# A decoder layer in fp32 on one core: other order of the first loads, one more filler product, and another rank for head norms and rotations

## The chip, the core and the metric

The kernel runs on one core of a Trainium2 chip. The metric is device time in microseconds of one execution; a run gives one such time, and one execution is profiled with the hardware's trace. Of the kernel before there are three runs and one profiled execution. TensorE multiplies matrices (PE in the profile; its weight loads are PEld), VectorE is DVE, ScalarE is ACT, GpSimd is POOL, and SyncE (SP) issues most loads.

## The reference

One layer on 256 rows of width 1024, in float32: a norm, one wide projection into three attention branches and their gates, three attentions, their merge, and a feed-forward part with a causal convolution.

```python
h = rmsnorm(x, mix_norm_g[l])
proj = h @ w_in[l]
qa, ka, va, qd, kd, vd, qm, graw = jnp.split(proj, split_at, axis=-1)
qa = rope(rmsnorm(heads(qa, N_MOBA_HEADS), moba_q_norm_g[l]), positions)
ka = rope(rmsnorm(heads(ka, N_MOBA_HEADS), moba_k_norm_g[l]), positions)
...
gates = jax.nn.sigmoid(graw.astype(jnp.float32)).astype(x.dtype).reshape(B, S, N_BRANCHES, D_MODEL)
mem_n = rmsnorm(mem, mem_norm_g[l])
mkv = (mem_n @ w_mem_kv[l]).reshape(B, N_MEM, 2, N_MEM_HEADS, HEAD_DIM)
...
o_a = moba_attention(qa, ka, va).reshape(B, S, MOBA_W) @ w_branch_moba[l]
o_d = dilated_attention(qd, kd, vd).reshape(B, S, DIL_W) @ w_branch_dil[l]
o_m = memory_attention(qm, mk, mv).reshape(B, S, MEM_W) @ w_branch_mem[l]
merged = gates[:, :, 0] * o_a + gates[:, :, 1] * o_d + gates[:, :, 2] * o_m
x = x + merged @ w_out[l]
h2 = rmsnorm(x, ffn_norm_g[l])
u = causal_depthwise_conv(h2 @ w_ffn_up[l], ffn_conv_w[l], ffn_conv_b[l])
u_gate, u_val = jnp.split(u, 2, axis=-1)
x = x + (jax.nn.silu(u_gate) * u_val) @ w_ffn_down[l]
```

`qa`, `ka`, `va` and `qd`, `kd`, `vd` are 384 columns wide (six heads of 64), `qm`, `mk`, `mv` 256; `graw` is 3072 wide, which the kernel takes in twelve gates of 256 columns (G0 to G11).

## The kernel before

Every product is made of three: both operands are split into a rounded part (`hi`) and the rest (`lo`), and `mm3` adds hi x hi, hi x lo and lo x hi in PSUM. A weight piece of up to 1024 columns is loaded by SyncE into one of six raw buffers (`load`, `NRAW`), rounded on ScalarE (`split_hi`), and the rest is taken on VectorE, or on ScalarE and a GpSimd DMA (`split_lo`). The columns of x are handled alike: `column_task` scales one column block of 128 by the norm's gain, the hi on ScalarE, the lo on VectorE (tile `T_x`). The factor of the norm itself is applied later, to the products (`rs_x`, `R`).

The order of the work is made by a planner when the program is built, not by hand and not on the chip. The class `Order` (methods `run` and `issue`) keeps a clock for each engine with estimated costs; every piece of work is a generator that yields stages, and at each step the ready stage with the lowest rank on the next engine is written out. The chip then runs each engine's list in that order. Where TensorE would be idle by that clock for over half a microsecond early on, `keep_busy` fills the time with products of a tile of ones, which nobody reads (`warm_...`).

The projections stand in the order va, vd, qa, G0, ka, G1, G2, mv, mk, and so on (`ORDER`). A k is a block of 128 of the 1024 rows of a weight; va is loaded in pieces of 1, 1, 2, 2, 2 k (`CUTS` and pieces of at most two k), the other projections in four pieces of two k. Products go piece by piece, both row halves t = 0, 1 for each: 12 products for a piece of two k.

The head of the program is written in `tile_layer` from line 1120: `LOADS` lists the first transfers, `x01` for the x columns 0 and 1 excluded, `g` for `small` (gains and positions), `w` for the next weight piece. The x columns went out on ScalarE's queue, the rest on SyncE's. There are eight semaphores for such transfers, taken in turn, so a transfer also waits for the one eight before it.

After a q or k projection `post_task` (line 592) does the head norms and the rotation, for t = 0 and then t = 1: squares on ScalarE (`sq_qa`), sums and a scalar step on VectorE (`hs_qa`), a power on GpSimd, the rotation on VectorE (`t_qa`: a product with `ropeA`, two with `ropeB`, an addition). After both halves, for each t: the scaling on VectorE (a `SCALAR_TENSOR_TENSOR` on `t_qa`), three transposes on TensorE (`tp_qa`), a copy on ScalarE. The stages of one task follow in this order, so the scaling of half 0 stands behind the rotation of half 1. Its rank was 20. Splitting a weight ranks by how many units ahead it is needed (`PRIO_SPLIT` with `urgency`, line 389): 0 for three units, then 12, 12, 22, 35, 40. The sums of squares of the memory rows (`junk_mem`, `mem_rows_task`) rank 23.

```python
PRIO_SPLIT = (0, 0, 0, 12, 12, 22, 35, 40)
...
        for t in range(NT):
            t1, rs, _ = parts[t]
            yield Stage("dve")
            dve.scalar_tensor_tensor(t1, t1, rstd[src, t][:, 0:1], rs, op0=ALU.mult, op1=ALU.mult)
            rows = t1.rearrange("p h d -> p (h d)")
            yield Stage("pe", bank_free("tp"))
```

Of the kernel before, what the change touches and what calls it, by code (L numbers as in the profile page):

```python
# [25 lines left out]
DH = 64  # L26
# [10 lines left out]
WARM = 4  # L37
RAW = 3
PRIO_SCALE = 11
CUTS = (0, 1, 2, 4, 8)  # L40
LOADS = "x01 g w x12 w x24 w x48 w w w"
SUMS = (4, 130, 5)
BACK = (1.5, 2.0)
SLACK = 0.6
# [193 lines left out]
def tile_layer(ctx: ExitStack, tc: tile.TileContext, io, out):  # L238
    nc = tc.nc
    od = Order(nc)  # L240
# [186 lines left out]
    task = {}  # L427
# [324 lines left out]
    def post_start(nm, accs):  # L752
        w = WID[nm]
        src = "mem" if nm in ("mk", "mv") else "x"
        if nm in ("va", "vd", "mv"):
            res[nm] = apool.tile([P, NT, w], F32, tag="v_" + nm, name="v_" + nm)
            task[nm] = od.add(v_task(accs, res[nm], w, src), 10)
        else:
            kind = ("qa", "ka", "qd", "kd", "qm", "mk").index(nm)
            res[nm] = apool.tile([P, w // P, S], F32, tag="T_" + nm, name="T_" + nm)  # L760
            task[nm] = chain["post"] = od.add(post_task(accs, nm, w // DH, kind, res[nm], src, done("rope"), chain["post"]), 20)
        if "mk" in task and "mv" in task and oT["there"] is None:
            oT["t"] = tpool.tile([P, KT, 2, S], F32R, tag="T8", name="oT")
            oT["there"] = 0.0
        for kind, names in enumerate(TRIPLES):
            if nm in names and all(n in task for n in names):
                attends(kind)
# [332 lines left out]
    def keep_busy(start):  # L1100

        if od.t["pe"] > 20.0 and not at["quiet"]:
            return
        n = int((start - od.t["pe"]) / (0.22 if od.t["pe"] > 7.0 else 0.43))
        if n < 1:
            return
        w, use = bank("sc", f"warm_{od.seq}_{start}")
        use["end"] = start
        for i in range(n):
            nc.tensor.matmul(w[:, 0, :P], ones, ones, start=True, stop=True)  # L1110

    od.idle = keep_busy
    with tc.manual_schedule():
# [6 lines left out]
        for w in LOADS.split():  # L1120
# [2 lines left out]
                at["dma"] += 0.06  # L1123
            elif w == "w":
                load(0.0, at["raw"] + 1)
            elif w[0] == "x":
                k0, k1 = int(w[1]), int(w[2])
                nc.scalar.dma_start(xcol[:, k0:k1, :], io["x_cols"][:, k0:k1, :])
                at["dma"] += 0.38 * (k1 - k0)
                for k in range(k0, k1):  # L1130
                    there[k] = at["dma"] + 1.2
# [82 lines left out]
```

## Time and profile before

| | us |
|---|---|
| median of three runs (lowest, highest) | 416.18 (415.67, 416.65) |
| profiled execution | 416.41 |
| its span, first to last instruction | 414.6 |
| PE busy | 406.4 (98%) |
| DVE busy | 302.6 (73%) |
| ACT busy | 270.9 (65%) |
| POOL busy | 58.9 (14%) |

All times below are microseconds from the start of the span. A row of the timeline gives start, duration, engine, line, operation, output and inputs, the count of instructions that follow one another without another between, and in brackets the idle time before it with what ended it. Line 105 is that of a helper which writes most operations out, so rows are told apart by their tiles; the tile names leave buffer numbers out. A matmul on fp32 without rounding (the fillers) shows as two instructions.

### The profile page before, as it was taken

To read this page: it belongs to the slowest core of one execution; us is meant where nothing else is said; L and a number is where in the kernel's file an instruction comes from. 1 tells how busy PE (TensorE), PEld (TensorE's weight loads), DVE (VectorE), ACT (ScalarE), POOL (GpSimd) and SP (SyncE) were. 2 spreads that over 40 slices of the span, in tenths; PEclk is the share of its full clock that TensorE was granted. 3 is DMA by queue.
4 is the path that set the end of the run, shared out by engine and by line. 5 is a ranking of instruction groups with operands and counts; after the bars stand their busy time and mean duration, and the time that the engine had idled before them with its cause. 6 is when DMAs were issued, how large, how long until landed. Compare 5 with 4: busy or idle time off the path is not lost.

```text
span 414.6 us, 7737 instructions
## 1 busy us (share of the span) xinstructions
PE 406.4 (98%) x2952; PEld 383.9 (93%) x2952; DVE 302.6 (73%) x601; ACT 270.9 (65%) x449; POOL 58.9 (14%) x62
## 2 busy tenths in 40 slices
PE   8999999999999999999999889999999999999996
PEld 7999899989989999999889889999999999888986
DVE  3998987675887676467977999999998778545301
ACT  4789765869986656957676958776667776443200
POOL 0001432312333103222008100000000000000000
PEclk9999999999999999999999999999999999999999
DMA  7999978577367877587696759676798687654001
GB/s 250 349 320 333 293 244 226 149 183 179 111 171 193 207 205 201 143 224 221 174 288 162 180 135 254 196 201 203 223 271 204 225 247 225 203 185 152 0 2 51
DMA packets 97557, 82.74 MB, mean 200 GB/s; under 512 B 2928, under 2 KB 85744, under 8 KB 97520
## 3 DMA queue, kind: packets, MB, share of 16 engines
q1 hardware_dynamic: 94496, 72.81, 58.2%
q0 software_dynamic: 2448, 8.39, 11.2%
q10 hardware_dynamic: 576, 1.05, 0.8%
q8 instruction: 23, 0.38, 0.4%
q14 instruction: 14, 0.11, 0.1%
HBM read 72.80 MB, written 1.05 MB: 178 GB/s over the span
## 4 chain that ended last, share of the span: by engine, by line
PE 91%; DVE 3%; ACT 3%; DMA 1%; issue 1%; SPq 0%; DVEq 0%; ACTq 0%
PE acc_u L105 27%; PE acc_g L105 16%; PE acc_d L105 15%; PE acc_o L105 5%; PE acc_va L105 3%; PE acc_qd L105 2%; PE acc_bd L105 2%; PE acc_ba L105 2%; PE acc_kd L105 2%; PE acc_vd L105 2%; PE acc_qa L105 2%; PE sc L105 2%; PE po L105 2%; PE acc_qm L105 1%; PE acc_mk L105 1%; PE acc_bm L105 1%
## 5 line engine op out<-in xcount | busy, mean ns | idle before, releaser
L105 PE MATMUL acc_u<-T_h,hi_up 128*128 128x256 f32 x512 | 91.4, 282 | 0.0
L105 PEld LDWEIGHTS acc_u<-T_h,hi_up 128*128 128x128 f32 x512 | 78.9, 189 | 0.0
L105 PE MATMUL acc_u<-T_h,lo_up 128*128 128x256 f32 x256 | 72.1, 282 | 0.0
L105 PE MATMUL acc_g<-T_x,hi_gate 128*128 128x256 f32 x384 | 71.7, 287 | 0.0
L105 PEld LDWEIGHTS acc_g<-T_x,hi_gate 128*128 128x128 f32 x384 | 59.5, 191 | 2.1 <-issue 1.8
L105 PE MATMUL acc_d<-hi_dn,gT 128*128 128x512 f32 (+1 forms) x220 | 57.0, 348 | 0.0
L105 PE MATMUL acc_g<-T_x,lo_gate 128*128 128x256 f32 x192 | 54.2, 282 | 0.0
L105 ACT ACTIVATE hi_up<-raw_up 128x1024 fp32r<-128x1024 f32 x44 | 46.0, 1053 | 4.0 <-PE acc_o L105 1.7
L105 PEld LDWEIGHTS acc_u<-T_h,lo_up 128*128 128x128 f32 x256 | 48.4, 189 | 0.0
L105 DVE TENSOR_TENSOR lo_up<-raw_up,hi_up 128x1024 fp32r<-128x1024 f32 x39 | 47.6, 1232 | 0.0
L105 DVE SCALAR_TENSOR_TENSOR y<-acc_u,conv,y 128x255 f32<-128x255 f32 x88 | 42.2, 481 | 7.3 <-ACT y L105 5.4
L105 PEld LDWEIGHTS acc_d<-hi_dn,gT 128*128 128x128 f32 x220 | 38.5, 189 | 5.6
L105 PE MATMUL acc_d<-lo_dn,gT 128*128 128x512 f32 (+1 forms) x110 | 38.3, 348 | 0.0
L105 DVE TENSOR_TENSOR lo_dn<-raw_dn,hi_dn 128x1024 fp32r<-128x1024 f32 x21 | 25.7, 1225 | 17.2 <-ACT hi_dn L105 16.9
L105 ACT ACTIVATE hi_dn<-raw_dn 128x1024 fp32r<-128x1024 f32 x22 | 23.3, 1057 | 22.4 <-PE acc_d L105 22.4
L105 PE MATMUL acc_u<-T_hu,hi_up 128*128 128x256 f32 x192 | 34.9, 284 | 2.6 <-DVE y L105 2.6
L105 PEld LDWEIGHTS acc_g<-T_x,lo_gate 128*128 128x128 f32 x192 | 36.6, 191 | 0.0
L105 DVE TENSOR_TENSOR lo_gate<-raw_gate,hi_gate 128x1024 fp32r<-128x1024 f32 x20 | 24.1, 1218 | 13.2 <-ACT hi_gate L105 13.1
L105 PEld LDWEIGHTS acc_u<-T_hu,hi_up 128*128 128x128 f32 x192 | 29.6, 189 | 2.9 <-ACT T_h L105 2.9
L105 ACT ACTIVATE y<-acc_u,conv 128x256 f32<-128x256 f32 x44 | 24.3, 560 | 10.9 <-PE acc_u L105 10.3
L105 ACT ACTIVATE hi_gate<-raw_gate 128x1024 fp32r<-128x1024 f32 x24 | 25.0, 1057 | 5.9 <-PE acc_g L105 2.4
L105 PE MATMUL acc_u<-T_hu,lo_up 128*128 128x256 f32 x96 | 27.1, 282 | 0.0
(279 smaller groups left out, 849.3 us busy)
## 6 DMA issues: line engine op xcount, KB each, us to landing
raw_up<-w_ffn_up SPq DMA_DIRECT2D x44, 512.0 KB, 4.8
raw_gate<-w_in SPq DMA_DIRECT2D x24, 512.0 KB, 5.5
raw_dn<-w_ffn_down SPq DMA_DIRECT2D x22, 512.0 KB, 4.5
raw_wo<-w_out SPq DMA_DIRECT2D x8, 512.0 KB, 4.4
lo_up<-raw_up POOLq DMA_DIRECT2D x5, 512.0 KB, 4.9
lo_gate<-raw_gate POOLq DMA_DIRECT2D x4, 512.0 KB, 5.1
raw_vd<-w_in SPq DMA_DIRECT2D x4, 384.0 KB, 7.0
raw_qa<-w_in SPq DMA_DIRECT2D x4, 384.0 KB, 7.7
```

Of the source, the lines that this page charges most:

```text
L105: return fn(*args, **kw)
```

## The change

It has four edits.

- `LOADS`: the x columns come in four transfers of two blocks. The first two stay on ScalarE's queue, the last two (`X46`, `X68`) go out on SyncE's queue, between weight pieces; the first weight pieces come one place earlier in the list.
- `CUTS` names a cut at 6. The pieces of va were at most two k already, so their sizes and number stay.
- `keep_busy`: in the first 7 us of the planner's clock one filler product more than before.
- `post_start`: the task of head norms and rotations has rank 8 in place of 20, so that it goes ahead of splits that are needed three or more units later, and of the memory rows' sums.

```diff
-CUTS = (0, 1, 2, 4, 8)
-LOADS = "x01 g w x12 w x24 w x48 w w w"
+CUTS = (0, 1, 2, 4, 6, 8)
+LOADS = "x02 g w w x24 w X46 w X68 w"
...
-            task[nm] = chain["post"] = od.add(post_task(accs, nm, w // DH, kind, res[nm], src, done("rope"), chain["post"]), 20)
+            task[nm] = chain["post"] = od.add(post_task(accs, nm, w // DH, kind, res[nm], src, done("rope"), chain["post"]), 8)
...
-        n = int((start - od.t["pe"]) / (0.22 if od.t["pe"] > 7.0 else 0.43))
+        n = int((start - od.t["pe"]) / 0.22) if od.t["pe"] > 7.0 else int((start - od.t["pe"]) / 0.43) + 1
...
-            elif w[0] == "x":
+            elif w[0] in "xX":
                 k0, k1 = int(w[1]), int(w[2])
-                nc.scalar.dma_start(xcol[:, k0:k1, :], io["x_cols"][:, k0:k1, :])
+                (nc.scalar if w[0] == "x" else nc.sync).dma_start(xcol[:, k0:k1, :], io["x_cols"][:, k0:k1, :])
```

The planner makes other lists of it for all engines up to the first gate products of G2; behind them the lists are the same. Three places show what moves.

ScalarE at the start of the program, before and then with the change (`sig` holds the x columns when they land, `T_x` the scaled ones, `raw_va` and `hi_va` a weight piece and its rounded part):

```order
L1128 DMA sig_85<-x_cols 128x256 x2
L1128 DMA sig_85<-x_cols 128x512
L1128 DMA sig_85<-x_cols 128x1024
L1132 ACT_TABLE_LOAD
L1132 ACTIVATE warm_90<-mhalf_76 128x1
L105 ACTIVATE T_x_113<-sig_85,small_71 128x256
L105 ACTIVATE hi_va_0_0_124<-raw_va_0_0_93 128x384
L105 ACTIVATE T_x_113<-sig_85,small_71 128x256
L105 ACTIVATE hi_va_0_0_131<-raw_va_0_0_96 128x384
L105 ACTIVATE T_x_113<-sig_85,small_71 128x256 x2
L105 ACTIVATE hi_va_0_0_162<-raw_va_0_0_99 128x768
L105 ACTIVATE T_x_113<-sig_85,small_71 128x256 x3
```

```order
L1128 DMA sig_85<-x_cols 128x512 x2
L1132 ACT_TABLE_LOAD
L1132 ACTIVATE warm_90<-mhalf_76 128x1
L105 ACTIVATE T_x_113<-sig_85,small_71 128x256 x2
L105 ACTIVATE hi_va_0_0_125<-raw_va_0_0_93 128x384
L105 ACTIVATE hi_va_0_0_129<-raw_va_0_0_95 128x384
L105 ACTIVATE T_x_113<-sig_85,small_71 128x256 x2
L105 ACTIVATE hi_va_0_0_161<-raw_va_0_0_98 128x768
L105 ACTIVATE T_x_113<-sig_85,small_71 128x256 x2
L105 ACTIVATE hi_va_0_0_186<-raw_va_0_0_101 128x768
L105 ACTIVATE T_x_113<-sig_85,small_71 128x256 x2
```

Two transfers in place of four are issued there, the scaling goes two blocks at a time, and two blocks now stand ahead of the first weight piece. On TensorE the fillers ahead of va's first product become seven for five, those ahead of its third piece four for six, and two ahead of its fourth piece are gone.

VectorE before the transposes of qa, before and then with the change (`hs_qa1` and `t1_qa1` belong to the half t = 1 of qa, `t1_qa0` to t = 0, `lo_gate_1` to G1, `lo_ka` to ka; the last row of each is the scaling of half 0):

```order
L105 TENSOR_REDUCE hs_qa1_607<-sq_qa1_606 128x6
L105 TENSOR_SCALAR hs_qa1_607<-hs_qa1_607,rs_x1_177 128x6
L105 TENSOR_TENSOR lo_gate_1_0_0_584<-raw_gate_1_0_0_451,hi_gate_1_0_0_583 128x1024
L105 SCALAR_TENSOR_TENSOR T_mem_114<-sig_85,small_71,T_mem_114 128x256
L105 TENSOR_TENSOR t1_qa1_608<-acc_qa_1_399,ropeA_80 128x384
L105 TENSOR_TENSOR t2_qa1_644<-acc_qa_1_399,ropeB_81 128x6x32 x2
L105 TENSOR_TENSOR lo_gate_1_0_128_614<-raw_gate_1_0_128_466,hi_gate_1_0_128_613 128x1024
L105 TENSOR_TENSOR t1_qa1_608<-t1_qa1_608,t2_qa1_644 128x384
L105 SCALAR_TENSOR_TENSOR t1_qa0_507<-t1_qa0_507,rs_x0_173,hs_qa0_506 128x384
```

```order
L105 TENSOR_REDUCE hs_qa1_585<-sq_qa1_584 128x6
L105 TENSOR_SCALAR hs_qa1_585<-hs_qa1_585,rs_x1_179 128x6
L105 TENSOR_TENSOR lo_ka_2_0_531<-raw_ka_2_0_407,hi_ka_2_0_530 128x768
L105 TENSOR_SCALAR rs_mem0_442<-rs_mem0_442 128x1
L105 TENSOR_SCALAR rs_mem1_445<-rs_mem1_445 128x1
L105 TENSOR_TENSOR lo_gate_1_0_0_595<-raw_gate_1_0_0_451,hi_gate_1_0_0_594 128x1024
L105 TENSOR_TENSOR t1_qa1_586<-acc_qa_1_396,ropeA_80 128x384
L105 TENSOR_TENSOR t2_qa1_629<-acc_qa_1_396,ropeB_81 128x6x32 x2
L105 TENSOR_TENSOR t1_qa1_586<-t1_qa1_586,t2_qa1_629 128x384
L105 SCALAR_TENSOR_TENSOR t1_qa0_489<-t1_qa0_489,rs_x0_175,hs_qa0_488 128x384
```

The split of ka's last piece now stands behind the reduction instead of ahead of it; a step of `T_mem` and the second gate split have left the stretch. On ScalarE the squares `sq_qa1` follow directly on the last sum of the memory rows, where a gate's rounding and the copy `sig` stood between. On GpSimd the power of `hs_qa1` goes ahead of the product of `sig` with `R`.

TensorE at the end of ka's products, before and then with the change (`hi_ka_2_0_533` and `hi_ka_2_0_530` are ka's last piece, `tp_qa_0` the transposes of qa's half 0, `acc_g1` gate 1):

```order
L105 MATMUL acc_ka_1_599<-hi_ka_2_0_533,T_x_113 128x384
L105 MATMUL acc_ka_1_599<-lo_ka_2_0_534,T_x_113 128x384
L105 MATMUL acc_ka_1_599<-hi_ka_2_0_533,T_x_113 128x384 x2
L105 MATMUL acc_ka_1_599<-lo_ka_2_0_534,T_x_113 128x384
L105 MATMUL acc_ka_1_599<-hi_ka_2_0_533,T_x_113 128x384
L105 MATMUL tp_qa_0_681<-ident_75,t1_qa0_507 128x128 x3
L105 MATMUL acc_g1_688<-T_x_113,hi_gate_1_0_0_583 128x256 x2
```

```order
L105 MATMUL acc_ka_1_597<-lo_ka_0_0_525,T_x_113 128x384
L105 MATMUL acc_ka_1_597<-hi_ka_0_0_524,T_x_113 128x384
L105 MATMUL tp_qa_0_656<-ident_75,t1_qa0_489 128x128 x3
L105 MATMUL acc_ka_0_577<-hi_ka_2_0_530,T_x_113 128x384
L105 MATMUL acc_ka_0_577<-lo_ka_2_0_531,T_x_113 128x384
L105 MATMUL acc_ka_0_577<-hi_ka_2_0_530,T_x_113 128x384 x2
```

The transposes stood between ka's last product and gate 1; now they stand ahead of ka's last piece, that is 12 products earlier. Those of half 1 move from 24 to 12 products into gate 1.

## Rows read from the trace of the kernel before

**Rows 1.** The page's chain of waits, shares of the span by engine.

```profile
PE 91%; DVE 3%; ACT 3%; DMA 1%; issue 1%; SPq 0%; DVEq 0%; ACTq 0%
```

**Rows 2.** Timeline of TensorE at the end of ka (start, us, engine, operation).

```profile
50.43 0.52 PE L105 MATMUL tp_qa<-ident,t_qa 128*128 128x128 f32 x3 [0.69 <-DVE t_qa L105]
50.70 0.48 PE L105 MATMUL acc_g<-T_x,hi_gate 128*128 128x256 f32 x2
```

**Rows 3.** Timeline of TensorE in the head of the program.

```profile
5.81 0.69 PE L105 MATMUL acc_va<-hi_va,T_x 128*128 128x384 f32 x1 [0.54 <-ACT hi_va L105]
...
9.89 0.52 PE L105 MATMUL acc_va<-hi_va,T_x 128*128 128x384 f32 x1
10.21 1.54 PE L1110 MATMUL warm_8.807152_184<-ones 128*128 128x128 f32 x12
...
14.06 0.42 PE L105 MATMUL acc_va<-hi_va,T_x 128*128 128x384 f32 x1
...
18.13 0.33 PE L105 MATMUL acc_va<-hi_va,T_x 128*128 128x384 f32 x1
```

**Rows 4.** Timeline of ScalarE: the third weight piece of va.

```profile
9.73 0.84 ACT L105 ACTIVATE hi_va<-raw_va 128x768 fp32r<-128x768 f32 x1 [1.14 <-DMA raw_va<-w_in]
```

**Rows 5.** Busy time by stretch; the last two columns: DMA share, GB/s.

```profile
0.00:7.20 7.20, 5.60 (x21) 5.00 (x22) 1.60 (x4) 2.81 (x5) 0.74 (x7) 1.00 0.69 185
0.00:8.50 8.50, 6.90 (x26) 6.04 (x26) 2.27 (x6) 4.03 (x8) 0.74 (x7) 1.00 0.74 218
...
18.00:21.00 3.00, 3.00 (x19) 3.00 (x18) 2.56 (x9) 1.54 (x5) 0.56 (x1) 1.00 0.92 284
```

**Rows 6.** Timeline of VectorE, 42.9 to 50.3 us.

```profile
42.97 0.95 DVE L105 TENSOR_TENSOR lo_ka<-raw_ka,hi_ka 128x768 fp32r<-128x768 f32 x1
43.84 0.21 DVE L105 TENSOR_SCALAR rs_mem<-rs_mem 128x1 f32<-128x1 f32 x1
...
44.42 0.55 DVE L105 TENSOR_REDUCE hs_qa<-sq_qa 128x6 f32<-128x384 f32 x1
45.01 0.62 DVE L105 TENSOR_SCALAR hs_qa<-hs_qa,rs_x 128x6 f32<-128x6 f32 x1
...
46.68 0.47 DVE L105 SCALAR_TENSOR_TENSOR T_mem<-sig,small,T_mem 128x256 fp32r<-128x256 f32 x1
...
48.07 1.21 DVE L105 TENSOR_TENSOR lo_gate<-raw_gate,hi_gate 128x1024 fp32r<-128x1024 f32 x1
...
49.67 0.60 DVE L105 SCALAR_TENSOR_TENSOR t_qa<-t_qa,rs_x,hs_qa 128x384 f32<-128x384 f32 x1
```

**Rows 7.** Timeline of ScalarE, 42 to 45 us.

```profile
42.02 0.19 ACT L105 ACTIVATION_READ_ACCUMULATOR junk_mem<-sig 128x1 f32 x1
...
43.42 0.58 ACT L105 ACTIVATE sig<-acc_g 128x512 f32<-128x512 f32 x1
43.90 0.48 ACT L105 ACTIVATE sq_qa<-acc_qa 128x384 f32<-128x384 f32 x1
44.27 1.06 ACT L105 ACTIVATE hi_gate<-raw_gate 128x1024 fp32r<-128x1024 f32 x1
```

**Rows 8.** One tile's instructions: the memory rows' two loads, 30 to 31 us.

```profile
L1080 SPq DMA_DIRECT2D sig<-mem x2: 458/820/1182, 29.7 to 30.2; - x2
...
DMA to landing us min/median/max: 9.5/10.0/10.4
```

**Rows 9.** Timelines of GpSimd and VectorE where they meet, 63 to 65 us.

```profile
63.01 1.34 POOL L105 TENSOR_TENSOR hs_ka<-hs_ka,mhalf 128x6 f32<-128x6 f32 x1 [1.67 <-DVE hs_ka L105]
64.34 1.28 POOL L105 TENSOR_TENSOR sig<-sig,R 128x512 f32<-128x512 f32 x1
...
63.88 0.56 DVE L105 TENSOR_TENSOR t_ka<-t_ka,t_ka 128x384 f32<-128x384 f32 x1
64.35 1.69 DVE L105 SCALAR_TENSOR_TENSOR t_ka<-t_ka,rs_x,hs_ka 128x384 f32<-128x384 f32 x1
```

**Rows 10.** Timeline of TensorE behind its longest wait in the feed-forward part.

```profile
239.82 0.48 PE L105 MATMUL acc_u<-T_hu,hi_up 128*128 128x256 f32 x2 [1.59 <-DVE y L105]
```

## The prediction

> **What bounds the kernel.** I read the chain of waits first: TensorE makes 91% of it [rows 1], so an edit is worth what it takes off TensorE's waits. The new order differs from the old one only up to the first gate products, some 60 us in; from there to the end every engine has the same list. So I price the change at one yardstick, the start of gate 1's products at 50.70 us [rows 2]. What they gain the end gains, since the later waits lie between engines that shift together.
>
> Before that point TensorE's timeline shows two losses. One is the head: first product at 5.81 us after 0.54 us of idling, products 0.32 us apart to 10.21 us, which is the 1.2 GHz level for 384 columns, then fillers. The 24 products from 14.06 to 18.13 us stand 0.177 apart, the 2.4 GHz level [rows 3]. TensorE had been busy since 5.81 us, but for two short waits, when the rate rose; the granted-clock column reads 1.00 throughout and does not show the step. The other loss is 0.69 us in front of the transposes of qa's first half (tp_qa_0), released by VectorE [rows 2].
>
> **The change, part by part.**
>
> *Loads.* The third weight piece (two k) arrived at 9.73 us, after ScalarE had waited 1.14 us for it [rows 4]. Before it or beside it went all 1.05 MB of x columns and 0.82 MB of small and weights, 1.87 MB. Now half of x stands behind it on SyncE's queue, so 1.34 MB suffice. The engines had moved 0.218 x 8.5 = 1.85 MB by 8.5 us and 0.185 x 7.2 = 1.33 MB by 7.2 us [rows 5], so the piece comes some 1.2 us earlier, near 8.5. Against that, the first two x columns come as one transfer, and both are scaled before the first weight piece is rounded: one step of about 0.4 us more and a later landing, so the first product starts near 6.5 us instead of 5.81. The fillers ahead of it cover the idle time: there are seven for five (one for the new rule, one for the later planned start). The five had ended 0.54 us ahead of 5.81, at 5.27 [rows 3]; two more, at half the rate of those at 10.21 (1.54 for six [rows 3]), take 1.0 and end near 6.3 us; they delay nothing. Behind the second weight piece four fillers stay of six, and the two ahead of the fourth piece go.
>
> If the rate rises near 10.2 us as before, the second batch of products ends near 10.7, four fillers take 1.0 (1.54 for six [rows 3]), then three batches of 12 x 0.177 = 2.1 us follow: va ends near 17.9 instead of 18.3 us. If the rate rises with the first products, the weights' second parts limit, and va ends near 16.7. TensorE is ahead by **g = 0.4 to 1.6 us**.
>
> *Ranks.* tp_qa_0 moves ahead of ka's last 12 products. TensorE comes there at 50.43 - 0.69 - 2.1 = 47.6 us, less g. By then VectorE has to have scaled qa's first half, which it began at 49.67 us [rows 6]. How early can it be now? The scaling stands behind the whole rotation of the second half, which starts from that half's squares on ScalarE (43.90 us). In the new list these squares follow directly on the four sums of the memory rows, the last of which ends at 42.02 + 0.19 = 42.21 us [rows 7]. And the sums go no earlier: the memory rows, issued at 29.7 and 30.2 us, landed 9.5 and 10.4 us later, at 39.2 and 40.6 [rows 8], and two of the sums follow the second landing. The queue holds the same bytes ahead of them as before. So the squares move from 43.90 to 42.24 us.
>
> From there VectorE's own list changes. From the reduction (44.42) to the scaling (49.67) it took 5.25 us. A step runs into the next by 0.08 (42.97 + 0.95 against 43.84), which I take off. Out go T_mem's step (0.47, net 0.39), the gate split at 48.07 (1.21, net 1.13) and the hold-up of a scalar step (0.62 against 0.21). In come ka's last split (0.87), two scalar steps of 0.15, and about 0.1 because the addition follows its operand at once. That leaves 4.6 us [rows 6]. The reduction, 0.52 behind its squares as before, starts at 42.75, the scaling at 47.35; it takes 0.60, and tp_qa_0 starts 0.16 later (49.67 + 0.60 to 50.43): 48.1. The gate split in between finds its input: squares, sig copy (0.58) and rounding of 1.06 us [rows 7] end near 44.2, and the split is due at 44.6.
>
> So TensorE waits there for 0.5 us **plus g**: what the head gains is spent in this wait. Transposes 0.27 (50.43 to 50.70), then 2.1 for the 12 products: gate 1 starts at 50.45 us against 50.70. That is -0.25 us, whatever the head gives.
>
> *GpSimd.* Its product sig x R now follows the power of hs_qa1. It can read only once the gate split has gone, at 45.7 us. It took 1.28 us at 64.34, and a vector step on two SBUF tiles that met it there took 1.69 instead of 0.60 us [rows 6, 9]. So it lasts until 47.0, and the addition, due near 46.9, may wait: 0.1 us, between 0 and 0.3.
>
> *The sum.* 416.41 us (the profiled execution: span 414.6 and 1.8 around it) - 0.25 + 0.1 = 416.26. The median of the three runs is 0.23 us lower, so I forecast **416.0**.
>
> *Bounds.* The DMA engines were busy for 0.92 of 18 to 21 us [rows 5]: 0.24 us that earlier issues could fill, and the memory rows would land that much earlier. With GpSimd's 0 to 0.3 this gives -0.5 to +0.05. A head that is slower than I say costs nothing until g is below -0.5.
>
> **Rivals.**
>
> *Faster: the memory rows come earlier.* If fewer, larger x transfers shorten the slow first microseconds of the loads (1.33 MB in 7.2 us, but 0.52 in the next 1.3 [rows 5]), the whole queue moves up. The gain ends where TensorE itself is late: tp_qa_0 at 47.6 - g without a wait puts gate 1 at 50.0 - g, a gain of 0.7 + g, 1.1 to 2.3 us, so 413.9 to 415.1; a part of it gives 415.1 to 415.6. At the later rate the first 7.2 us would have needed 3.3, so there is room. Against: the rows land behind some 12 MB that stay as they were. Faster by over 0.83 us: 0.28.
>
> *Slower: GpSimd gets in ahead of the gate split.* If sig x R starts before the split of gate 1's first half, that split waits out the product, and with it the scaling: 1.28 us, gate 1 near 51.7, about 1 us late: 417.2. The point is whether the power ends before 44.6 us: it can't start before 43.6 and takes 1.34 [rows 9], so the margin is 0.35 us. A power itself holds nothing up by the rows: the addition at 63.88 took 0.56 us inside the power of 63.01 to 64.35 [rows 9]. The Trainium skill, SBUF — State Buffer, section SBUF: two separate sides, says otherwise: a GpSimd instruction that gets the port pair it shares with VectorE keeps it for the whole instruction, and a vector step with two SBUF inputs fully blocks. By that rule the power would take the port near 44.3 and the gate split wait until 45.7, 1.1 us late: about 417.1. The row at 63.88 speaks against it. Chance of both: 0.12.
>
> *Slower: the longer wait costs the clock.* TensorE's wait grows from 0.69 to between 0.9 and 2.1 us. If its rate fell to the 1.2 GHz level for a stretch like that of the first 12 products, they would cost 12 x (0.32 - 0.177) = 1.7 us: 417.7. But after a wait of 1.59 us two products took 0.48 us [rows 10], as the first two of gate 1 did [rows 2]. The Trainium skill, TensorE: Matmul & The Clock Gate, section HAM oscillation — how this bites in real kernels, warns that waits for data between groups of products bring the half rate back; no row here shows that after a wait of this length. Chance 0.03.
>
> *It does not do what it says.* If the loads gain nothing and the ranks only trade places on VectorE, the time is 416.2: inside "same".
>
> **The numbers.** A measurement of this kernel can tell about 0.2% (0.83 us) from no change: faster is below 415.35, slower above 417.0. A small gain or none, my forecast, has 0.57; faster 0.28; slower 0.15. The range 415.0 to 417.0 takes in the bounds and the nearer part of the faster case.
>
> **What would show it.** In the new profile: first product near 6.5 us with little idle time ahead, third weight piece rounded near 8.5 to 8.8, va's end earlier by 0.4 to 1.6; the sums of the memory rows still from 39.2 to 42.2 us; the squares of qa's second half near 42.3, the scaling near 47.4; a wait of 0.9 to 2.1 us in front of tp_qa_0, released by VectorE; gate 1 at 50.4 to 50.6. I am wrong if the memory rows' sums move by over half a microsecond, if tp_qa_0 finds no wait, or if the time from gate 1 to the end changes.

## The result, and the profile after

The changed kernel takes **414.27 us** (median of 4 runs, 414.0 to 414.65), beside 416.09 us (415.67 to 416.65) for the kernel before: a ratio of 0.9948 (95% interval 0.9929 to 0.9967), or 1.8 us. That is faster and lies below the forecast range of 415.0 to 417.0. The profiled execution took 414.52 us, its span is 412.7 us for 414.6 before. TensorE's share of the chain of waits rose from 91% [rows 1]:

```profile
PE 93%; ACT 2%; DVE 2%; DMA 1%; issue 0%; SPq 0%; ACTq 0%
```

I follow the yardstick of the prediction, the start of gate 1's products. TensorE's timeline, changed kernel (start, us, engine, line, operation), answers to [rows 2, 3]:

```profile
2.92 2.48 PE L1110 MATMUL rm_5.796666666666667_139<-ones 128*128 128x128 f32 x14
6.68 0.44 PE L105 MATMUL acc_va<-hi_va,T_x 128*128 128x384 f32 x1 [1.27 <-ACT hi_va L105]
...
9.59 1.05 PE L1110 MATMUL warm_8.807152_189<-ones 128*128 128x128 f32 x8
10.40 0.42 PE L105 MATMUL acc_va<-hi_va,T_x 128*128 128x384 f32 x1
...
17.04 0.33 PE L105 MATMUL acc_vd<-hi_vd,T_x 128*128 128x384 f32 x1
...
46.02 0.34 PE L105 MATMUL acc_ka<-hi_ka,T_x 128*128 128x384 f32 x1
46.43 0.52 PE L105 MATMUL tp_qa<-ident,t_qa 128*128 128x128 f32 x3
...
48.87 0.40 PE L105 MATMUL acc_g<-T_x,hi_gate 128*128 128x256 f32 x2
```

va ends (that is, the first product of vd starts) at 17.04 instead of 18.30 us, 1.26 earlier. Products here follow one another 0.17 us apart, so tp_qa_0 starts 46.43 - 46.02 - 0.17 = 0.24 us after the product ahead of it would release TensorE. In the kernel before the same subtraction gives 50.43 - 49.40 - 0.17 = 0.86 us (the label says 0.69, since it counts from the product's modelled end):

```profile
49.40 0.34 PE L105 MATMUL acc_ka<-hi_ka,T_x 128*128 128x384 f32 x1
```

The prediction had this wait grow, to 0.5 + 1.26 = 1.8 us by the label. Gate 1 starts at 48.87 instead of 50.70: -1.83 us. From there to the end it is 412.7 - 48.87 = 363.8 us, for 414.6 - 50.70 = 363.9 before. So the whole gain lies ahead of gate 1: 1.26 in the head and 0.57 between there and gate 1, where the wait at tp_qa_0 shrank by 0.62.

What made the wait go is on ScalarE and VectorE (timelines of the changed kernel; compare [rows 4, 6, 7]):

```profile
8.67 0.83 ACT L105 ACTIVATE hi_va<-raw_va 128x768 fp32r<-128x768 f32 x1
...
34.26 0.51 ACT L105 ACTIVATE T_mem<-sig,small 128x256 fp32r<-128x256 f32 x1 [0.16 <-DMA sig<-mem_cols]
...
36.25 1.57 ACT L105 ACTIVATE hi_ka<-raw_ka 128x768 fp32r<-128x768 f32 x2
37.72 0.62 ACT L105 ACTIVATE junk_mem<-sig 128x512 bf16<-128x512 f32 x1
...
40.51 0.19 ACT L105 ACTIVATION_READ_ACCUMULATOR junk_mem<-sig 128x1 f32 x1
40.60 0.47 ACT L105 ACTIVATE sq_qa<-acc_qa 128x384 f32<-128x384 f32 x1
```

```profile
41.11 0.55 DVE L105 TENSOR_REDUCE hs_qa<-sq_qa 128x6 f32<-128x384 f32 x1
...
42.95 1.22 DVE L105 TENSOR_TENSOR lo_gate<-raw_gate,hi_gate 128x1024 fp32r<-128x1024 f32 x1
...
45.67 0.61 DVE L105 SCALAR_TENSOR_TENSOR t_qa<-t_qa,rs_x,hs_qa 128x384 f32<-128x384 f32 x1
```

The sums of the memory rows run from 37.72 to 40.70 us instead of 39.24 to 42.21. The squares follow them directly, as forecast, but at 40.60 instead of 42.24, and the scaling at 45.67 instead of 47.35. What the sums stood behind in the kernel before, on ScalarE:

```profile
35.78 0.91 ACT L105 ACTIVATE T_mem<-sig,small 128x256 fp32r<-128x256 f32 x2 [0.18 <-DMA sig<-mem_cols]
...
39.24 0.61 ACT L105 ACTIVATE junk_mem<-sig 128x512 bf16<-128x512 f32 x1
```

In both kernels ScalarE's last wait ahead of the sums is for the memory columns, and from there it has work without a gap: 39.24 - 35.78 = 3.46 us before, 37.72 - 34.26 = 3.46 in the changed kernel. So the first sum is 1.52 us earlier because the second half of the memory columns landed 1.52 us earlier. The memory rows have to be there too, and they came earlier as well, which the prediction had ruled out for its main case. Their two loads (one tile's instructions, 28.9 to 30.2 us):

```profile
L1080 SPq DMA_DIRECT2D sig<-mem x2: 645/698/752, 29.0 to 29.8; - x2
...
DMA to landing us min/median/max: 8.6/8.8/9.1
```

They were issued 0.4 to 0.7 us earlier and landed after 9.1 us at most instead of 10.4 [rows 8]: near 37.6 and 38.9, instead of 39.2 and 40.6. In the kernel before each landing is within 0.1 us of the moment at which ScalarE comes to that row's sums; in the changed kernel the rows are there 0.2 to 0.3 us ahead of ScalarE.

### The profile page after: what moved, and what is told of

Its sections match the earlier page's. It is cut to its first block, busy times and chain, and to the rows that moved or that the text cites. A ratio compares the mean times of both kernels' runs of the same rounds, so it can differ in the third digit from the quotient of the medians.

```text
span 412.7 us, 7727 instructions
## 1 busy us (share of the span) xinstructions
PE 404.2 (98%) x2948; PEld 381.6 (92%) x2948; DVE 302.5 (73%) x601; ACT 271.6 (66%) x449; POOL 60.5 (15%) x62
## 4 chain that ended last, share of the span: by engine, by line
PE 93%; ACT 2%; DVE 2%; DMA 1%; issue 0%; SPq 0%; ACTq 0%
PE acc_u L105 27%; PE acc_g L105 17%; PE acc_d L105 15%; PE acc_o L105 5%; PE acc_qd L105 2%; PE acc_bd L105 2%; PE acc_va L105 2%; PE acc_ba L105 2%; PE acc_kd L105 2%; PE acc_qa L105 2%; PE acc_vd L105 2%; PE acc_ka L105 2%; PE sc L105 2%; PE po L105 2%; PE acc_qm L105 1%; PE acc_mk L105 1%
## 5 line engine op out<-in xcount | busy, mean ns | idle before, releaser
L105 ACT ACTIVATE y<-acc_u,conv 128x256 f32<-128x256 f32 x44 | 24.4, 561 | 10.8 <-PE acc_u L105 10.2
```

Of the source, the lines that this page charges most:

```text
L105: return fn(*args, **kw)
```

## The experiments

The question is why the memory columns and rows came earlier, and what each of the three parts gives. The table holds one profiled execution of each kernel (times are starts from the timelines; "wait" is TensorE's labelled idle time ahead of tp_qa_0; an empty place means that none is labelled) and the medians of the timed runs. The kernel before had medians of 416.60 to 416.63 us beside the twelve.

| kernel | first product (idle before) | va's end | memory columns issued | first sum | scaling of qa, half 0 | wait | gate 1 | median, us (n) | ratio, 95% interval |
|---|---|---|---|---|---|---|---|---|---|
| before | 5.81 (0.54) | 18.30 | 27.75 | 39.24 | 49.67 | 0.69 | 50.70 | | |
| changed | 6.68 (1.27) | 17.04 | 26.66 | 37.72 | 45.67 | | 48.87 | 414.27 (4) | 0.9929 to 0.9967 |
| e1_loads | 6.29 (1.30) | 16.97 | 26.59 | 38.10 | 48.22 | 0.61 | 49.25 | 415.03 (10) | 0.9949 to 0.9976 |
| e2_rank | 6.37 (1.10) | 18.36 | 28.07 | 39.13 | 48.00 | | 50.16 | 417.69 (12) | 1.0017 to 1.0044 |
| e3_filler | 6.29 (1.30) | 18.49 | 27.96 | 39.40 | 49.85 | 0.67 | 50.87 | 416.25 (12) | 0.9985 to 1.0014 |
| e5_loads_rank | 6.59 (1.55) | 17.93 | 27.55 | 38.56 | 46.53 | | 49.74 | 414.88 (10) | 0.9947 to 0.9972 |
| f_again | 6.18 | 16.61 | 26.40 | 37.16 | 45.12 | | 48.31 | 414.18 (6) | 0.9935 to 0.9964 |
| e4_loads_filler | 6.66 (0.54) | 16.79 | 26.41 | 37.20 | 47.31 | | 48.34 | 414.79 (7) | 0.9945 to 0.9973 |
| f_delay | 6.94 (0.82) | 19.63 | 29.26 | 40.04 | 48.47 | 0.27 | 51.69 | 416.90 (12) | 0.9998 to 1.0025 |
| f_rope14 | 6.45 (1.28) | 16.49 | 27.00 | 39.10 | 44.35 | 0.26 | 48.81 | 416.17 (12) | 0.9969 to 0.9998 |
| g_fill9 | 6.46 | 16.96 | 26.60 | 37.78 | 45.72 | 0.20 | 48.93 | 414.65 (6) | 0.9937 to 0.9971 |
| g_delay_R | 6.92 (1.44) | 20.94 | 26.19 | 40.52 | 48.58 | | 53.03 | 418.5 (1) | |
| h_rank20 | 7.06 (0.95) | 17.02 | 26.77 | 37.52 | 47.63 | | 48.66 | 414.83 (12) | 0.9949 to 0.9977 |
| h_after3 | 6.53 (1.34) | 16.65 | 26.27 | 37.12 | 45.08 | | 48.27 | 414.27 (6) | 0.9927 to 0.9963 |

**One part at a time.** e1_loads takes the loads and the cut alone:

```diff
-CUTS = (0, 1, 2, 4, 8)
-LOADS = "x01 g w x12 w x24 w x48 w w w"
+CUTS = (0, 1, 2, 4, 6, 8)
+LOADS = "x02 g w w x24 w X46 w X68 w"
...
-                nc.scalar.dma_start(xcol[:, k0:k1, :], io["x_cols"][:, k0:k1, :])
+                (nc.scalar if w[0] == "x" else nc.sync).dma_start(xcol[:, k0:k1, :], io["x_cols"][:, k0:k1, :])
```

> Only the new order of the first loads and the cut at 6; rank 20 and the old filler rule (six fillers ahead of the first product by the planned start, where the changed kernel has seven). Theory A (the loads start the head earlier, and the memory rows follow because raw buffers come free earlier): third weight piece rounded near 8.7 us, va's end near 17.0 instead of 18.3, the sums of the memory rows near 37.7 instead of 39.2, but tp_qa_0 still behind ka's last products with a wait of about 0.7 us, so gate 1 near 49.4 and the time 1.2 to 1.4 us below before. Theory B (the early rise of TensorE's rate comes from the seventh filler): products stay 0.32 us apart until after 10 us, va's end at 17.9 to 18.3, time within 0.4 us of before. Theory C (the rank alone brought the memory rows' sums forward): sums stay at 39.2.

The times of theory A hold: va ends at 16.97, the sums start at 38.10, and the old wait stays, 0.61 us. The median is 1.6 us below before, where the changed kernel was 1.8 us below in the first comparison and 2.4 in two later ones (f_again, h_after3): the loads alone bring most of the gain. Which part of that edit does it (fewer transfers, half of x on SyncE's queue, weights earlier in the list) no run separates. Theory C falls, since the sums moved without the rank. Theory B falls too: six fillers, and products 0.18 apart soon after the start. The reason that theory A gives is not shown by this run: the memory rows were issued at 29.64 us, no earlier than before (29.69), and the sums still came 1.14 us earlier, as the memory columns did (issued 1.16 earlier).

e2_rank takes the rank alone:

```diff
-            task[nm] = chain["post"] = od.add(post_task(accs, nm, w // DH, kind, res[nm], src, done("rope"), chain["post"]), 20)
+            task[nm] = chain["post"] = od.add(post_task(accs, nm, w // DH, kind, res[nm], src, done("rope"), chain["post"]), 8)
```

> Only the rank 8 for head norms and rotations; loads and fillers as before. Theory A: the head and the landing of the memory rows are those of before (sums from 39.2 to 42.2 us), the scaling of qa's first half near 47.4, a wait of 0.4 to 0.6 us in front of tp_qa_0, gate 1 near 50.45: 0.2 to 0.3 us below before. Theory C (the rank brought the sums forward): sums near 37.7, no wait at tp_qa_0, gate 1 near 50.0, 0.6 to 0.7 us below before.

The sums stay at 39.13, as forecast, and gate 1 comes 0.54 us earlier than before, without the wait of 0.4 to 0.6 us that was expected (here the planner put the transposes only six products ahead of gate 1). But the kernel is slower, by 0.31%: the planner now sends one part of lo_mv through GpSimd's queue, where the kernel before has VectorE make it, and TensorE waits for it. TensorE's timeline of e2_rank:

```profile
62.04 0.28 PE L105 MATMUL acc_mv<-hi_mv,T_mem 128*128 128x256 f32 x1
64.36 0.39 PE L105 MATMUL acc_mv<-lo_mv,T_mem 128*128 128x256 f32 x1 [2.04 <-DMA lo_mv<-raw_mv]
```

A rank in the planner has paid out 0.54 us at one place and taken back 2.04 us at another. In the changed kernel that part of lo_mv stands on VectorE, and there is no such wait.

e3_filler takes the filler alone (six ahead of the first product):

```diff
-        n = int((start - od.t["pe"]) / (0.22 if od.t["pe"] > 7.0 else 0.43))
+        n = int((start - od.t["pe"]) / 0.22) if od.t["pe"] > 7.0 else int((start - od.t["pe"]) / 0.43) + 1
```

> Only one filler product more ahead of the first product (six for five); loads and rank as before. Theory B (the sixth filler is what raises TensorE's rate early): the products of va stand 0.18 us apart from the first on, the second batch ends near 9.5 instead of 10.2 us, and the third, with six fillers at the high rate, starts near 10.7 to 11.0 instead of 11.5: 0.5 to 0.8 us below before. Theory A: the rate rises where it did, near 10 us, and the time is that of before within 0.2 us.

No difference (0.9985 to 1.0014). TensorE's rate did rise early in this profile, and it changed nothing: va ends at 18.49 us. With the old loads the third weight piece sets that end, and an early rate only waits for it: this piece was rounded at 9.96 us, and TensorE waited 0.51 us for its rest, to 11.85.

e5_loads_rank is the changed kernel without the filler line of e3_filler.

> Loads and rank as in the changed kernel, without its extra filler (six ahead of the first product instead of seven). Theory A: as the changed kernel, va's end near 17.0, tp_qa_0 almost without a wait, gate 1 near 48.9, 1.7 to 1.9 us below before. Theory B: products 0.32 us apart until after 10 us, va's end at 17.9 to 18.3, tp_qa_0 with a wait of about half a microsecond, 0.3 to 0.6 us below before.

The median lies with e1_loads (414.88 and 415.03). The profile shows something else: va ends at 17.93, because the granted clock fell to 0.50 in the head. Busy time by stretch of e5_loads_rank (the granted clock is the third column from the right):

```profile
7.00:8.00 1.00, 0.85 (x5) 0.82 (x5) 0.78 (x3) 1.00 (x3) 0.00 (x0) 0.80 1.06 400
8.00:9.00 1.00, 1.00 (x5) 1.00 (x4) 0.96 (x4) 1.00 (x3) 0.00 (x0) 0.50 1.07 396
...
10.00:11.00 1.00, 1.00 (x6) 1.00 (x5) 1.00 (x4) 1.00 (x3) 0.00 (x0) 0.50 1.06 375
```

va's end and the first sum are both 0.9 us later than in the changed kernel (17.93 for 17.04, 38.56 for 37.72): a first hint that these loads follow TensorE.

**Do the loads follow the compute?** f_delay holds TensorE back in the head and leaves the list of loads as it is:

```diff
         if n < 1:
             return
+        if od.t["pe"] > 7.0:
+            n += 12
```

> The changed kernel with 12 more filler products behind the second batch of va (sixteen for four), so that TensorE is held back by 12 x 0.107 = 1.3 us from 9.6 us on; all loads and all other lists as they are. Theory A (buffers come free earlier because the compute is earlier, and so the later loads): with va's end near 18.3 the fourth and later weight pieces are issued later, the sums of the memory rows start at 38.6 to 39.2 instead of 37.7. Theory E (the larger first transfers alone put the queue ahead): sums still at 37.5 to 37.9, and TensorE comes 1.3 us late to a scaling of qa that is long done. In both the time is 1.0 to 1.4 us above the changed kernel.

The delay is larger than the expectation says: a filler is two records, so the twelve took 24 x 0.109 = 2.6 us, and va ends 19.63 - 17.04 = 2.6 us later. The memory columns are issued 2.6 us later too (29.26 for 26.66), the memory rows as well (31.58 for 28.98), and their sums start at 40.04 instead of 37.72: ScalarE itself comes later to them, and the third sum waits 0.50 us more for the second row. Theory E falls for these loads: they come 2.6 us later, in the same order, because TensorE does. It stands for the loads ahead of them. SyncE's queue with ka's first two pieces, in the kernel before, the changed kernel and f_delay:

```profile
24.75 2.43 SPq L305 DMA_DIRECT2D raw_ka<-w_in  x2
...
23.98 2.12 SPq L305 DMA_DIRECT2D raw_ka<-w_in  x2
...
24.21 4.49 SPq L305 DMA_DIRECT2D raw_ka<-w_in  x2
```

In f_delay the first of the two is issued at 24.21, still 0.54 us ahead of the kernel before, although va ends 1.33 us later than there; the second one only at 28.32. So up to ka's first piece the queue is earlier than before even with TensorE late, and from the second on it follows TensorE. Gate 1 moves by 2.82 us and the median is 2.7 us above the changed kernel's beside it (f_again).

The path of that delay can be read on four engines. SyncE's queue, changed kernel:

```profile
25.73 0.37 SPq L305 DMA_DIRECT2D raw_ka<-w_in  x1
26.15 0.46 SPq L1066 DMA_DIRECT2D conv<-conv  x1
26.66 0.90 SPq L1070 DMA_DIRECT2D sig<-mem_cols  x2
```

VectorE, changed kernel: the piece whose end frees the slot for raw_ka, 0.03 us ahead of its issue (24.74 + 0.96 = 25.70):

```profile
24.74 0.96 DVE L105 TENSOR_TENSOR lo_qa<-raw_qa,hi_qa 128x768 fp32r<-128x768 f32 x1
```

The same piece in f_delay, 27.34 + 0.96 = 28.30, and raw_ka's issue at 28.32:

```profile
27.34 0.96 DVE L105 TENSOR_TENSOR lo_qa<-raw_qa,hi_qa 128x768 fp32r<-128x768 f32 x1 [2.50 <-ACT hi_qa L105]
```

It waits for ScalarE, and ScalarE stands, in the order of its list, behind R, a copy that waits for a TensorE product (f_delay):

```profile
26.29 0.28 ACT L105 ACTIVATE R<-tp_Rx 128x128 f32<-128x128 f32 x1 [2.61 <-PE tp_Rx L105]
26.46 0.84 ACT L105 ACTIVATE hi_qa<-raw_qa 128x768 fp32r<-128x768 f32 x1
```

g_delay_R cuts that link: f_delay with the copy ranked behind the roundings.

```diff
-            task[f"R{t}"] = od.add(row_scale_task("x", t), 9)
+            task[f"R{t}"] = od.add(row_scale_task("x", t), 32)
```

> The delayed kernel (12 more fillers behind the second batch of va) with the row-scale copies R ranked 32 instead of 9, so that on ScalarE the rounding of qa no longer stands behind a copy that waits for TensorE's tp_Rx (2.61 us in the delayed kernel). Theory A in its full form (TensorE late, ScalarE late in order behind tp_Rx, raw slots free late, SyncE's queue late with raw_ka, the memory columns and the memory rows): with that link cut, qa's second rounding starts near 23.5 to 24.0 instead of 26.46, the memory columns are issued near 26.5 to 27.2 instead of 29.26, the memory rows near 28.7 to 29.8 instead of 31.6, though va ends as late as with the delay alone (18.2 to 18.6). Rival (the slots are held by TensorE's own products in another place): the memory columns stay at 28.7 to 29.4. The whole time is no evidence here, since the planner's lists change up to the middle of the program.

In this execution TensorE is later still (va ends at 20.94; its granted clock, too, fell to 0.50 near 8 us). Yet the rounding starts at 23.30 and the memory columns are issued at 26.19, 3.1 us earlier than in f_delay, earlier even than in the changed kernel. The link is the right one in these lists. The second half of the expectation failed: the memory rows are issued at 34.08 instead of 28.7 to 29.8. SyncE's queue and ScalarE of g_delay_R say why:

```profile
26.19 0.90 SPq L1070 DMA_DIRECT2D sig<-mem_cols  x2
27.19 6.84 SPq L305 DMA_DIRECT2D raw_ka<-w_in  x2
34.08 0.93 SPq L1080 DMA_DIRECT2D sig<-mem  x2
```

```profile
28.42 0.58 ACT L105 ACTIVATE v_vd<-acc_vd,rs_x 128x384 f32<-128x384 f32 x1 [3.55 <-PE acc_vd L105]
...
31.80 0.83 ACT L105 ACTIVATE hi_qa<-raw_qa 128x768 fp32r<-128x768 f32 x1
```

The last piece of qa now stands behind another step that needs TensorE (v_vd), and the queue waits for its slot. It is the same coupling, one step further on.

Over the table the coupling is nearly a constant. In the nine profiles with the new loads other than f_rope14 (another list) and g_delay_R, the time from va's end to the memory columns' issue lies between 9.62 and 9.79 us, while va's end itself moves over 3.0 us (16.61 to 19.63). With the old loads it is 9.45 to 9.71 us, but by other lists. The path in the kernel before, on TensorE, ScalarE and VectorE:

```profile
23.50 0.38 PE L105 MATMUL tp_Rx<-diag_x,ones 128*128 128x128 f32 x2
...
24.09 0.58 ACT L105 ACTIVATE v_va<-acc_va,rs_x 128x384 f32<-128x384 f32 x1
24.56 0.84 ACT L105 ACTIVATE hi_qa<-raw_qa 128x768 fp32r<-128x768 f32 x1
...
25.82 0.96 DVE L105 TENSOR_TENSOR lo_qa<-raw_qa,hi_qa 128x768 fp32r<-128x768 f32 x1
```

TensorE and ScalarE, changed kernel:

```profile
23.27 0.38 PE L105 MATMUL tp_Rx<-diag_x,ones 128*128 128x128 f32 x2
...
23.70 0.28 ACT L105 ACTIVATE R<-tp_Rx 128x128 f32<-128x128 f32 x1 [0.25 <-PE tp_Rx L105]
23.87 2.30 ACT L105 ACTIVATE hi_qa<-raw_qa 128x768 fp32r<-128x768 f32 x3
```

So between these two kernels TensorE's earlier head is the smaller part. tp_Rx starts only 0.23 us earlier, since the planner put it 36 products behind va's end instead of 30, and R 0.22 (23.70 for 23.92). The piece of qa that frees the slot is 1.08 us earlier (24.74 for 25.82): 0.47 because v_va no longer stands between R and the rounding, and 0.39 because VectorE takes the piece up 0.03 us after its rounding instead of 0.42. This split is read from the rows; no run tests the order of v_va or of VectorE's steps alone. The rows also say how far the coupling reaches: ScalarE waits for tp_Rx for 1.62 us before and 0.25 in the changed kernel, and with the link cut (g_delay_R) the memory columns go out only 0.47 us earlier than there. By these rows a still earlier head would pull them forward by about that much on this path, and no more.

**What the rank is worth beside the loads.** e4_loads_filler and h_rank20 are the changed kernel with rank 20, each timed beside a repetition of the changed kernel (f_again, h_after3; no edit).

```diff
-task[nm] = chain["post"] = od.add(post_task(accs, nm, w // DH, kind, res[nm], src, done("rope"), chain["post"]), 8)
+task[nm] = chain["post"] = od.add(post_task(accs, nm, w // DH, kind, res[nm], src, done("rope"), chain["post"]), 20)
```

> Loads and filler as in the changed kernel, with the old rank 20. If the rank is worth what the wait at tp_qa_0 shows (0.61 us with the loads alone, none in the changed kernel): that wait is back with 0.6 to 0.7 us, gate 1 at 49.3 to 49.4 at the early rate, and the median is 0.4 to 0.7 us above the changed kernel. If the rank only lets other work take its place: median within 0.2 us of the changed kernel. The sums of the memory rows start within 0.5 us of 37.7 at the early rate in either case.

> The changed kernel once more. Theory D (by execution, and not by the number of fillers, TensorE's rate rises near 4.6 or near 10.2 us; the old loads can't use the early rise, since the third weight piece sets va's end at 18.3 to 18.5 either way; the new ones can, 17.0 against 17.9): va ends at 17.0 if the products stand 0.18 apart from the first on, and at 17.8 to 18.0 if they stand 0.32 apart until 10.2; the times of single runs spread over about 1.5 us, median 414.3 to 414.9. Theory B (the seventh filler raises the rate): va's end at 17.0 every time, median 414.3 or below, all runs within 0.8 us.

> Loads and filler with the old rank 20 again, beside the changed kernel, for the worth of the rank. If it is worth a wait at tp_qa_0 only in executions in which the memory columns land late: median 0.2 to 0.6 us above the changed kernel run beside it, and a profile with gate 1 at 48.3 without a wait or at 49.0 to 49.4 with one of 0.5 to 0.7. If it is worth nothing: medians within 0.2 us.

> The changed kernel a third time, as the partner of the two timed kernels beside it: median 414.1 to 414.6, gate 1 at 48.3 to 48.9 with va's end at 16.6 to 17.1; in an execution with idle time before the first product and a rate that falls back, 17.9 and 49.7.

The medians of rank 20 are 0.6 us higher both times (414.79 for 414.18, 414.83 for 414.27), though the intervals of the ratios overlap, and without the filler the difference is 0.15 us (e1_loads, e5_loads_rank). The profiles don't show 0.6. With rank 20 the scaling came at 47.31 and 47.63, just in time, so the wait that e4_loads_filler was expected to show was not there, and gate 1 started at 48.34 and 48.66, for 48.31 and 48.27. From gate 1 to the end rank 20 takes 0.1 to 0.2 us more (spans of 412.3 and 412.6 us, for 412.1 and 412.1). Of the new loads with rank 20 only e1_loads, where the sums began at 38.10, shows TensorE waiting, 0.61 us. That the rank pays in executions in which the memory columns land late fits these profiles, but it is argued, not shown, since only one execution of each kernel has a trace, and its time lay below the median of its runs.

**Attempts at a faster version.** f_rope14 lets the chain of the rotation tables start later, so that VectorE has the third weight piece's rest first.

```diff
-ROPE_AT = 5.0
+ROPE_AT = 14.0
```

> The changed kernel with the rotation tables' chain allowed from 14 us on instead of 5 us: VectorE then has no cast and product (9.27 to 9.83) ahead of the rest of the third weight piece. If that rest bounds the head at the early rate, as 10.84 in the changed kernel says, its product starts 0.4 to 0.55 us earlier, va ends at 16.5 to 16.6, and 0.2 to 0.5 us of it reach the end, if nothing later turns late (the lists differ to the first gate products, and one part of lo_mv goes by GpSimd's queue). If the fillers or ScalarE bound the head, va ends at 17.0 and the time is that of the changed kernel. A new wait in front of acc_mv, as with the rank alone, would cost up to 2 us.

va ends at 16.49, 0.28 us sooner after the start of the third batch than in the changed kernel (16.49 - 10.13 for 17.04 - 10.40), about half of what was expected. It costs more: one part of lo_mv goes by GpSimd's queue again. TensorE's waits in f_rope14:

```profile
PE acc_mv L105 <- DMA lo_mv<-raw_mv: 1.0, 1, 1.0
```

The median is 2.0 us above the changed kernel's beside it. Of the 1.6 us between the two profiles (spans of 413.7 and 412.1 us) that wait is 1.0, and 0.5 lies ahead of gate 1 (48.81 for f_again's 48.31); the other 0.4 of the medians isn't settled.

g_fill9 puts nine fillers ahead of the first product instead of seven.

```diff
-        n = int((start - od.t["pe"]) / 0.22) if od.t["pe"] > 7.0 else int((start - od.t["pe"]) / 0.43) + 1
+        n = int((start - od.t["pe"]) / 0.22) if od.t["pe"] > 7.0 else int((start - od.t["pe"]) / 0.43) + 3
```

> The changed kernel with two more fillers ahead of the first product (nine for seven). Theory F (with idle time of over a microsecond between the fillers and the first product the rate can fall back, as with loads and rank alone, granted 0.50 from about 7.6 to 10.9 us after 1.55 us of idle time; fillers up to the first product prevent it): the fillers end between 5.8 and 6.9 us, the products stand 0.18 apart from the first on, va ends at 16.6 to 17.2, and the single runs lie within 1.0 us with a median at or below that of the changed kernel run beside it. Rival: at the low rate nine fillers take until 2.93 + 9 x 0.45 = 7.0 us and hold the first product up by 0.3 to 0.8 us, of which up to that reaches the end: median 0.2 to 0.6 us above.

The idle time ahead of the first product is gone and the rate stays up, but va's end (16.96) and the median (414.65, beside 414.27) are no better, and the runs spread over 1.2 us, where at most 1.0 was expected (the changed kernel's beside it spread over 1.6). None of the kernels tried beats the changed one.

## Why the prediction was wrong

**The loads: right.** The third weight piece was rounded at 8.67 us (forecast 8.5 to 8.8), the first product came at 6.68 (6.5), and va's end was 1.26 us earlier, within g = 0.4 to 1.6. Both branches were seen: 17.93 us with the low rate until about 11 us (e5_loads_rank; forecast 17.9, for a rise near 10.2), 16.61 to 17.04 with the early one (forecast 16.7). That the fillers would cover the idle time was wrong: they ended at 5.40, because the rate rose while they ran, and TensorE then stood for 1.27 us, at no cost in this execution. A slip without weight: 10.7 + 1.0 + 3 x 2.1 is 18.0 us and not 17.9, so the low end of g was 0.3.

**The chain behind the squares: right.** Reduction 0.51 us after the squares (forecast 0.52), 4.56 us from there to the scaling (4.6), 0.76 from the scaling to tp_qa_0 (0.76).

**The step that failed** is "And the sums go no earlier", with its reason "The queue holds the same bytes ahead of them as before" and its result "That is -0.25 us, whatever the head gives". The bytes are the same, but the queue does not run by bytes alone. SyncE issues in order, a weight piece is issued only when a slot is free, and the slots come free by ScalarE's and VectorE's splits. The new lists have these splits earlier: ka's first piece went out 0.77 us earlier (23.98 for 24.75), and f_delay shows that this needs no earlier end of va; from ka's second piece on the splits stand behind the copy R, which waits for TensorE, and moved by 1.08 us, partly with TensorE and more by another order. The memory columns were issued 1.09 us earlier and landed 1.52 earlier; why their way from issue to landing took 0.4 us less stays open. The memory rows landed near 37.6 and 38.9 us instead of 39.2 and 40.6. I had also taken that landing for what releases the sums; ScalarE's list, which waits for the memory columns, does in the changed kernel, and nearly ties with it in the kernel before. The sums came 1.52 us earlier (37.72 for 39.24), and the wait at tp_qa_0, which I had grow to 1.8 us, shrank to 0.24. What I priced at -0.25 us was -1.83. The row that should have warned me was there: ScalarE's wait of 1.62 us for tp_Rx in the kernel before, just ahead of qa's roundings:

```profile
23.92 0.28 ACT L105 ACTIVATE R<-tp_Rx 128x128 f32<-128x128 f32 x1 [1.62 <-PE tp_Rx L105]
```

**The bound failed with it.** I took a busy share of 0.92 in 18 to 21 us [rows 5] as 0.24 us that could still be filled. The share says how long the DMA engines had something to do, not how much they moved. Busy time by stretch, changed kernel:

```profile
0.00:7.20 7.20, 4.79 (x23) 4.34 (x23) 1.59 (x4) 2.91 (x5) 0.74 (x7) 1.00 0.70 202
...
18.00:21.00 3.00, 3.00 (x19) 3.00 (x18) 2.52 (x8) 1.45 (x5) 0.56 (x1) 1.00 1.02 339
```

The first 7.2 us moved 0.12 MB more than before (202 for 185 GB/s), and 18 to 21 us another 0.17 MB (339 for 284), together 0.8 us at the 384 GB/s that both kernels moved from 7.2 to 18 us.

**The rivals.** The one that the memory rows come earlier, with a chance of 0.28, is what happened: its bound, 0.7 + g = 1.96 us, holds the measured 1.83. But its reason, faster first microseconds, is the small part (0.12 MB, 0.3 us at 384 GB/s), and the slots stand nowhere in it; that it held the number is in part luck. Had I let the sums move with g, the gain would have been 0.15 + g instead of 0.15: 414.4 to 415.6, with the measured 414.27 just below it. That the change does nothing, and both slower cases, are out. Sig x R began at 43.95, near the gate split's end, and held up nothing: the addition took its usual 0.56 us, where the sum had put in 0.1 for it. The power did overlap the split. GpSimd, and the step of VectorE that ran when the power began, changed kernel:

```profile
41.84 0.95 DVE L105 TENSOR_TENSOR lo_ka<-raw_ka,hi_ka 128x768 fp32r<-128x768 f32 x1
42.01 1.97 POOL L105 TENSOR_TENSOR hs_qa<-hs_qa,mhalf 128x6 f32<-128x6 f32 x1 [0.31 <-DVE hs_qa L105]
```

The split of 42.95 to 44.17 began inside it, shared 1.03 us with it and kept its usual length (1.22 us, 1.21 in [rows 6]). It was the power that took 1.97 us instead of the 1.34 [rows 9] that I had put in: ka's split was running when it began, and it ended 42.01 + 1.97 - (41.84 + 0.95) = 1.19 us after that split. By the Trainium skill, SBUF — State Buffer, section SBUF: two separate sides, the split of 42.95 would have waited until the power's end; this trace contradicts it for this pair, as the row at 63.88 did. A power that starts while a split runs does look held up by it: in the kernel before this power began at 45.71, took 2.24 us and also ended 1.19 us after the split (45.55 to 46.76) that it met. The clock did not fall at tp_qa_0, where no long wait was left; so what a wait of 0.9 to 2.1 us would have cost was not tested.

**After gate 1** nothing changed, as forecast: 363.8 us for 363.9.

## What to carry to other kernels

A transfer's landing is not pinned by the bytes ahead of it when the queue issues in order and each issue waits for a buffer: follow the buffer's release back to the engine that frees it, and see whether that engine waits, in its own order, for the stage that you are making faster. If it does, the two move together, as far as that wait reaches, and what looks like a wall moves with the gain. When a time stays or moves, look at all that has to be there for it: here a landing and an engine's own list met at the same moment, and only one of them was priced. And try a planner's rank by itself and with its companions: the same rank gave 2 us away at a place 12 us further on, through a choice of the planner that no line of the diff names.

## What the runs showed of the hardware that I had not expected

**TensorE's rate in the head differs between executions of the same list.** e2_rank and the kernel before have the same head. In the profile of the kernel before, products stood 0.32 us apart until 10.2 us [rows 3]; in e2_rank they stand at the 2.4 GHz spacing soon after the start (the next product behind the last row starts at 7.58, so 0.34 us for two):

```profile
2.92 2.34 PE L1110 MATMUL warm_5.374288_135<-ones 128*128 128x128 f32 x10
6.37 0.44 PE L105 MATMUL acc_va<-hi_va,T_x 128*128 128x384 f32 x1 [1.10 <-ACT hi_va L105]
...
7.24 0.51 PE L105 MATMUL acc_va<-hi_va,T_x 128*128 128x384 f32 x2
```

It is worth nothing with the old loads (va's end 18.30 and 18.36). With the new ones va's end differs by 0.9 to 1.3 us between e5_loads_rank, where the rate was low from about 7.6 to 11 us, and the three profiles of the changed kernel. The granted-clock column reads 1.00 in both, so a low level from the start doesn't show there; the spacing does.

**A rate once risen can fall back.** In the two executions with 1.55 and 1.44 us of idle time ahead of the first product (e5_loads_rank, g_delay_R) the granted clock fell to 0.50 near 8 us and stayed there to about 11 us; in the other twelve, with 0 to 1.34 us, the column shows no fall. Two cases don't make a rule. The Trainium skill, TensorE: Matmul & The Clock Gate, section HAM oscillation — how this bites in real kernels, says that waits for data between groups of products bring the half rate back; these two heads agree with it, though the fall comes 1.0 to 1.2 us after the products have begun (6.59 and 6.92 us). Why executions differ, no run here shows.
